# Hybrid attention and Hyena encoder on one core: the low parts of 72 weight chunks move from GpSimd to VectorE, 40 softmax divisions move from VectorE to ScalarE, eight rotary-table products get a second factor

## The chip, the cores and the metric

One core of a Trainium2 chip runs the whole program. The metric is the device time of one execution in microseconds (us). PE is TensorE, DVE is VectorE, ACT is ScalarE, POOL is GpSimd, SP is SyncE, whose queue starts most transfers here.

## The reference, cut to what matters

Two layers over 272 tokens (16 learned meta tokens and 256 of the input) of width 2048, all in fp32. Each layer has a latent attention with 8 heads beside a Hyena group (three streams, a short convolution, a long convolution by FFT), one output projection, and a SwiGLU network of inner width 5632. The meta tokens are dropped at the end, so the second layer computes mostly 256 tokens.

```
p = hn @ w_in[l]
a = mla(p[..., :o1], p[..., o1:o2], p[..., o2:o3], ...)   # 8 heads
y = hyena(p[..., o3:], ...)                               # v*x1, long conv, *x0
mix = concat([rmsnorm(a, attn_out_g[l]), rmsnorm(y, hy_out_g[l])])
h = h + mix @ w_out[l]
...
s = einsum('bqhd,bkhd->bhqk', qb, k) * scale
p = softmax(s)                                            # exp, then / sum
o = einsum('bhqk,bkhd->bqhd', p, v)
```

## The kernel before, in words

**Products in three parts.** TensorE multiplies fp32 numbers in a rounded form (fp32r). To keep the precision each operand is split: a high part, which ScalarE writes by a cast to fp32r (line 122), and a low part, which is the source minus the high part (line 123). `mm3` (lines 167 to 170) then gives three matmuls for each 128x128 block of a weight: high times high (L168), weight-high times activation-low (L169) and weight-low times activation-high (L170). So TensorE can't finish a block before both parts of its weight are there.

**The stream of weights.** All large weights pass through `Parts`. `load_raw` has SP load one tile of 128 rows and up to 2048 columns into one of four raw buffers; `more` splits it in chunks of 512 columns, four to a `u` tile (columns of w_in) and two to a `wo` tile (w_out), into six high and six low buffers. The transfers, the casts and the low parts are each held in the stream's order by a chain. The low part is made on VectorE, except where a chunk's number is in the argument `pool`: those go to GpSimd and are in no chain. For the 24 `u` tiles of a layer that argument is the table's entry `uw`: chunks 1 and 3 in layer 0 (48 instructions), chunk 1 in layer 1 (24). VectorE makes the other 120.

**What sets the order.** `drive` advances the stream (`fill`: 24 `u` tiles, then 16 `wo` tiles for the attention's half of w_out) one tile a round and, beside it, a number of threads: the latents, four pairs of heads (`pair`), the convolution's tables (`conv_tables`) and four convolution groups. The table `SCHED` (lines 47 to 50) says at which round each starts and how many rounds lie between its steps. From that the framework's scheduler lays out one fixed program for each engine, so an instruction that is late holds up all that stands behind it on the same engine.

**A `u` tile** (`stream_tile`) takes 48 matmuls into one of three PSUM buffers. L608 on VectorE evicts it (times the norm's factor), L609 on ScalarE and L610, L612 on VectorE make the short convolution. The third tile after it needs its PSUM buffer.

**Softmax** (`softmax`, called by `scores` in `pair`): VectorE scales the scores (L478), takes the row maximum (L479) and scales it (L480), ScalarE makes the exponential with the row sum (L481), VectorE the reciprocal (L482) and the product with it (L483). Then TensorE transposes p (`turn`, L562). There are three blocks of queries a head in layer 0 (24 calls) and two in layer 1 (16).

**Rotary tables** (`rope_tables`, L406 and L407): GpSimd multiplies the cosine and sine tables by a gain for each partition; two calls a layer, so eight instructions.

**The convolution** begins with `conv_tables`: ScalarE and VectorE split the tables of the Fourier transform, `ftw` into `fth` and `ftl`, `frw` into `fr`, `itw` last. `conv_group` makes filters (`fb`, `rt`, `ru`, `av`, of which L751, L753 and L759 are on GpSimd), their parts (`kl`, `ar`, `br`) and spectra (`KR`, `KP`).

Of the kernel before, what the change touches and what calls it, by code (L numbers as in the profile page):

```python
# [11 lines left out]
AF = mybir.ActivationFunctionType  # L12
ALU = mybir.AluOpType
# [31 lines left out]
NFIRST = 1  # L45
QV = 3
SCHED = (
    dict(lat=1, nets=0, pair=(4, 4, 11, 11), tab=16, conv=(14, 15, 17, 18), gq=1, gp=2, gt=3, gl=1, gw=2, gm=1, gf=3, gk=2, gu=3, gy=2, uw=(1, 3), fe=1),
    dict(lat=0, nets=0, pair=(2, 6, 9, 11), tab=14, conv=(12, 17, 17, 22), gq=2, gp=2, gt=1, gl=1, gw=2, gm=1, gf=1, gk=2, gu=2, gy=2, uw=(1,), fe=1),
)  # L50


# [1 line left out]
def tile_hybrid_encoder(ctx: ExitStack, tc: tile.TileContext, a: dict):  # L54
    nc = tc.nc
# [33 lines left out]
    def HT(name, dt=F32):  # L89
        return heap.tile([P, T], dt, tag="t1", name=nm(name))  # L90

    def SM(name):
        return smallp.tile([P, 1], F32, tag="s1", name=nm(name))
# [16 lines left out]
    cosT = cpool.tile([P, T], F32, name="cosT")  # L110
    sinT = cpool.tile([P, T], F32, name="sinT")

    def pc(l, c):
        return par[:, l * NP + c : l * NP + c + 1]
# [239 lines left out]
    for l in range(NL):  # L354
# [48 lines left out]

        def rope_tables(cg, cgs):
            cg_, sg_ = HT("cg"), HT("sg")
            nc.gpsimd.tensor_scalar(out=cg_, in0=cosT, scalar1=pc(l, cg), scalar2=None, op0=ALU.mult)  # L406
            nc.gpsimd.tensor_scalar(out=sg_, in0=sinT, scalar1=pc(l, cgs), scalar2=None, op0=ALU.mult)  # L407
            return cg_, sg_

        def rope(src, tabs, t0):  # L410
# [28 lines left out]
        for c, (c0, c1) in enumerate(CH):  # L439
            n = c1 - c0  # L440
# [21 lines left out]
        def latents():  # L462
            at["qla"] = latent_norm(qlc, qls, q0, C_GQL, 512, "ql")
            ktab = rope_tables(C_KR, C_KRS)
            at["qtab"] = rope_tables(C_QR, C_QRS)
            krot = rope(kr, ktab, 0)
            khi, klo = HT("krh", F32R), HT("krl", F32R)
            split(khi, klo, krot)
            at["krot"] = (khi, klo)
            at["krsq"] = HT("krsq")  # L470
            nc.scalar.activation(at["krsq"], kr, AF.Square)
            yield

        def softmax(ps, n, rk, rq, name):

            mx, sm = SM("mx"), SM("sm")
            p = HT(name)
            nc.vector.tensor_tensor(out=p[:n], in0=ps[:n, :T], in1=rk[:n], op=ALU.mult)  # L478
            nc.vector.tensor_reduce(out=mx[:n], in_=p[:n], axis=AX.X, op=ALU.max)  # L479
            nc.vector.tensor_scalar(out=mx[:n], in0=mx[:n], scalar1=rq[1][:n], scalar2=None, op0=ALU.mult)  # L480
            nc.scalar.activation(p[:n], p[:n], AF.Exp, bias=mx[:n], scale=rq[0][:n], accum_out=sm[:n])  # L481
            nc.vector.reciprocal(out=sm[:n], in_=sm[:n])  # L482
            nc.vector.tensor_scalar(out=p[:n], in0=p[:n], scalar1=sm[:n], scalar2=None, op0=ALU.mult)  # L483
            return p

        def pair(pr):
# [53 lines left out]
            def scores(j):  # L540
                ps_ = []
                kh, kl = ke[j][:2]
                qh, ql = qe[j][:2]
                for c, (s0, s1) in enumerate(qch):
                    n = s1 - s0
                    o = j * nq + c
                    ps = PA("s")
                    pw = ps[:n, :T]
                    MM(pw, lhsT=qr[j][:, s0:s1], rhs=at["krot"][0], start=True, stop=False)
                    MM(pw, lhsT=qr[j][:, s0:s1], rhs=at["krot"][1], start=False, stop=False)  # L550
                    mm3(pw, qh[:, s0:s1], ql[:, s0:s1], kh, kl, False, True)
                    ps_.append(softmax(ps, n, rk[j], (rq[:, o : o + 1], rqn[:, o : o + 1]), "p"))
                return ps_
# [566 lines left out]
```

## Time and profile before

| | |
|---|---|
| median of 3 runs | 2399.38 us (2398.22 to 2399.62) |
| the profiled execution's own time | 2399.11 us |
| its span | 2397.3 us |
| mean granted TensorE clock | 0.994 of full speed |
| PE / DVE / ACT / POOL busy | 98% / 69% / 54% / 20% |

The span is the stretch between the first and the last instruction on record; 1.8 us of the profiled execution lie around it. The program has, in this order, a start (to about 60 us), the streams with attention of layer 0 (to 260 us), its convolution (to 320 us), the rest of w_out and the wide network (to 1280 us), and the same again for layer 1 from 1280 us, with its streams and attention to 1460 us and its convolution to 1540 us. Everything that the change touches directly lies between 60 and 320 us and between 1280 and 1540 us.

To read it: the busy time of an engine in a stretch beside that stretch's length says how much room it has; the waits of PE say who came last when PE stood still; the granted clock says at which of its two levels, 2.4 GHz (1.0) and 1.2 GHz (0.5), TensorE ran, as a mean over the stretch.

### The profile page before, as it was taken

To read this page: it belongs to the slowest core of one execution; us is meant where nothing else is said; L and a number is where in the kernel's file an instruction comes from. 1 tells how busy PE (TensorE), PEld (TensorE's weight loads), DVE (VectorE), ACT (ScalarE), POOL (GpSimd) and SP (SyncE) were. 2 spreads that over 40 slices of the span, in tenths; PEclk is the share of its full clock that TensorE was granted. 3 is DMA by queue.
4 is the path that set the end of the run, shared out by engine and by line. 5 is a ranking of instruction groups with operands and counts; after the bars stand their busy time and mean duration, and the time that the engine had idled before them with its cause. 6 is when DMAs were issued, how large, how long until landed. Compare 5 with 4: busy or idle time off the path is not lost.

```text
span 2397.3 us, 48489 instructions
## 1 busy us (share of the span) xinstructions
PE 2357.8 (98%) x19026; PEld 2336.5 (97%) x19026; DVE 1644.7 (69%) x2997; ACT 1295.8 (54%) x2609; POOL 474.0 (20%) x564
## 2 busy tenths in 40 slices
PE   8999899999999999999999999899999999999999
PEld 7999899999999999999999999899999999999999
DVE  6898998755555555555667899997666655556555
ACT  6877565644444444444556776556445454445443
POOL 2645732211111100110013444431000010000000
PEclk9999999999999999999999999999999999999999
DMA  6434333555555555555454443246555555555554
GB/s 240 159 124 144 116 110 110 208 176 176 176 176 176 176 176 176 176 176 176 159 194 161 157 149 122 90 131 214 192 179 192 181 189 185 185 189 181 193 170 149
DMA packets 72938, 402.03 MB, mean 168 GB/s; under 512 B 8195, under 2 KB 18692, under 8 KB 33156
## 3 DMA queue, kind: packets, MB, share of 16 engines
q1 hardware_dynamic: 72152, 398.38, 49.0%
q8 instruction: 149, 2.44, 0.4%
q14 instruction: 81, 0.66, 0.1%
q10 hardware_dynamic: 556, 0.55, 0.1%
HBM read 396.79 MB, written 2.10 MB: 166 GB/s over the span
## 4 chain that ended last, share of the span: by engine, by line
PE 92%; DVE 5%; issue 1%; ACT 1%; DMA 1%; SPq 0%; DVEq 0%; ACTq 0%
PE fd L169 7%; PE fu L168 7%; PE fg L168 7%; PE fd L170 7%; PE fd L168 7%; PE fu L170 7%; PE fg L170 7%; PE fg L169 7%; PE fu L169 7%; PE u L168 3%; PE u L169 3%; PE u L170 3%; PE wo L168 3%; PE wo L169 3%; PE wo L170 2%
## 5 line engine op out<-in xcount | busy, mean ns | idle before, releaser
L169 PE MATMUL fd<-al,wdh 128*128 128x272 f32 (+1 forms) x1408 | 401.5, 285 | 0.0
L168 PE MATMUL fu<-nfh,wuh 128*128 128x272 f32 (+1 forms) x1408 | 401.1, 285 | 0.0
L168 PE MATMUL fg<-nfh,wgh 128*128 128x272 f32 (+1 forms) x1408 | 400.9, 285 | 0.0
L170 PE MATMUL fd<-ah,wdl 128*128 128x272 f32 (+1 forms) x1408 | 400.8, 285 | 0.0
L170 PE MATMUL fg<-nfh,wgl 128*128 128x272 f32 (+1 forms) x1408 | 400.5, 284 | 0.0
L170 PE MATMUL fu<-nfh,wul 128*128 128x272 f32 (+1 forms) x1408 | 400.5, 284 | 0.0
L168 PE MATMUL fd<-ah,wdh 128*128 128x272 f32 (+1 forms) x1408 | 400.2, 284 | 0.0
L169 PE MATMUL fu<-nfl,wuh 128*128 128x272 f32 (+1 forms) x1408 | 400.1, 284 | 0.0
L169 PE MATMUL fg<-nfl,wgh 128*128 128x272 f32 (+1 forms) x1408 | 400.0, 284 | 0.0
L123 DVE TENSOR_TENSOR wgl<-wg,wgh 128x512 fp32r<-128x512 f32 x352 | 244.1, 694 | 211.7 <-ACT wgh L122 203.4
L123 DVE TENSOR_TENSOR wdl<-wd,wdh 128x512 fp32r<-128x512 f32 x352 | 245.6, 698 | 199.1 <-ACT wdh L122 187.0
L122 ACT CAST wdh<-wd 128x512 fp32r<-128x512 f32 x352 | 218.5, 621 | 282.2 <-PE fd L169 263.1
L123 DVE TENSOR_TENSOR wul<-wu,wuh 128x512 fp32r<-128x512 f32 x352 | 260.5, 741 | 160.8 <-ACT wuh L122 154.6
L122 ACT CAST wgh<-wg 128x512 fp32r<-128x512 f32 x352 | 218.6, 621 | 262.0 <-PE fg L169 140.7
L122 ACT CAST wuh<-wu 128x512 fp32r<-128x512 f32 x352 | 218.5, 621 | 257.1 <-PE fu L169 138.6
L898 POOL TENSOR_TENSOR gt<-gt,up 128x272 f32<-128x272 f32 (+1 forms) x88 | 96.9, 1101 | 1113.5 <-ACT wuh L122 1053.1
L169 PEld LDWEIGHTS fu<-nfl,wuh 128*128 128x128 f32 x1408 | 265.6, 189 | 0.1
L169 PEld LDWEIGHTS fg<-nfl,wgh 128*128 128x128 f32 x1408 | 265.6, 189 | 0.0
L168 PEld LDWEIGHTS fd<-ah,wdh 128*128 128x128 f32 x1408 | 265.6, 189 | 0.0
L168 PEld LDWEIGHTS fu<-nfh,wuh 128*128 128x128 f32 x1408 | 265.5, 189 | 0.0
L168 PEld LDWEIGHTS fg<-nfh,wgh 128*128 128x128 f32 x1408 | 265.5, 189 | 0.0
L169 PEld LDWEIGHTS fd<-al,wdh 128*128 128x128 f32 x1408 | 265.4, 188 | 0.0
(372 smaller groups left out, 5871.6 us busy)
## 6 DMA issues: line engine op xcount, KB each, us to landing
wg<-w_gate SPq DMA_DIRECT2D x88, 1024.0 KB
wu<-w_up SPq DMA_DIRECT2D x88, 1024.0 KB
wd<-w_down SPq DMA_DIRECT2D x64, 1024.0 KB
u<-w_in SPq DMA_DIRECT2D x48, 1024.0 KB
wo<-w_out SPq DMA_DIRECT2D x64, 512.0 KB
wd<-w_down SPq DMA_DIRECT2D x32, 768.0 KB
ql<-w_in SPq DMA_DIRECT2D x8, 1024.0 KB
wq<-w_qk SPq DMA_DIRECT2D x8, 1024.0 KB
```

Of the source, the lines that this page charges most:

```text
L122: h_ = nc.scalar.copy(out=hi, in_=src)
L123: l_ = (nc.gpsimd if pool else nc.vector).tensor_tensor(out=lo, in0=src, in1=hi.bitcast(F32), op=ALU.subtract)
L168: MM(ps, lhsT=lh, rhs=rh, start=first, stop=False)
L169: MM(ps, lhsT=lh, rhs=rl, start=False, stop=False)
L170: MM(ps, lhsT=ll, rhs=rh, start=False, stop=last)
L898: nc.gpsimd.tensor_tensor(out=t[:, w], in0=t[:, w], in1=u[:, w], op=ALU.mult)
```

## The change

Three edits. The table's `uw` becomes empty in both layers, so that the 72 low parts that GpSimd made are made on VectorE, and join its chain. The softmax's L483 becomes a copy on ScalarE with the reciprocal as its scale (40 instructions). The eight products of the rotary tables get a second factor of 1.0.

```
-    dict(lat=1, ..., gy=2, uw=(1, 3), fe=1),
-    dict(lat=0, ..., gy=2, uw=(1,), fe=1),
+    dict(lat=1, ..., gy=2, uw=(), fe=1),
+    dict(lat=0, ..., gy=2, uw=(), fe=1),
...
-            nc.gpsimd.tensor_scalar(out=cg_, in0=cosT, scalar1=pc(l, cg), scalar2=None, op0=ALU.mult)
-            nc.gpsimd.tensor_scalar(out=sg_, in0=sinT, scalar1=pc(l, cgs), scalar2=None, op0=ALU.mult)
+            nc.gpsimd.tensor_scalar(out=cg_, in0=cosT, scalar1=pc(l, cg), scalar2=1.0, op0=ALU.mult, op1=ALU.mult)
+            nc.gpsimd.tensor_scalar(out=sg_, in0=sinT, scalar1=pc(l, cgs), scalar2=1.0, op0=ALU.mult, op1=ALU.mult)
...
-            nc.vector.tensor_scalar(out=p[:n], in0=p[:n], scalar1=sm[:n], scalar2=None, op0=ALU.mult)
+            nc.scalar.activation(p[:n], p[:n], AF.Copy, scale=sm[:n])
```

No other line differs, but the scheduler lays the engines' programs out anew. Three places show how; + is the changed kernel, - the one before.

DVE in layer 0, ahead of the eviction of one `u` tile (`u_4039`), among the transform's tables (`ftl`); `ul_4411` is the low part of a chunk of a later `u` tile, `wol_4558` that of a chunk of the first `wo` tile:

```order
+L123 TENSOR_TENSOR ul_4411<-u_4400,uh_4410 128x512
+L123 TENSOR_TENSOR ul_4415<-u_4400,uh_4414 128x512
 L123 TENSOR_TENSOR ftl_3949<-ftw_3551,fth_3948 128x256
-L123 TENSOR_TENSOR ul_4231<-u_4220,uh_4230 128x512
 L123 TENSOR_TENSOR ftl_3953<-ftw_3553,fth_3952 128x256
+L123 TENSOR_TENSOR wol_4558<-wo_4555,woh_4557 128x512
 L123 TENSOR_TENSOR ftl_3957<-ftw_3555,fth_3956 128x256
 L123 TENSOR_TENSOR ftl_3961<-ftw_3557,fth_3960 128x256
+L123 TENSOR_TENSOR wol_4562<-wo_4555,woh_4561 128x512
 L123 TENSOR_TENSOR ftl_3965<-ftw_3559,fth_3964 128x256
 L608 TENSOR_TENSOR u_4039<-u_3972,nmr_505 128x272
-L123 TENSOR_TENSOR ul_4403<-u_4400,uh_4402 128x512
```

The low parts of the stream stand further ahead against the convolution's work than before, and four of 128x512 stand in this piece ahead of the eviction where one stood.

ACT in layer 0, in the softmax of the first heads; `uh_2358` and its like are casts of the stream, `uc_2061` is the short convolution of a `u` tile:

```order
-L122 CAST uh_2219<-u_2205 128x512
 L122 CAST uh_2358<-u_2356 128x512
+L122 CAST uh_2362<-u_2356 128x512
+L483 ACTIVATE p_1911<-p_1911,sm_1910 128x272
+L609 ACTIVATE uc_2061<-u_2060,par 128x272
 L481 ACTIVATE p_1926,sm_1925<-p_1926,mx_1924,rq_1703 128x272
-L122 CAST uh_2362<-u_2356 128x512
+L122 CAST uh_2366<-u_2356 128x512
 L481 ACTIVATE p_1941,sm_1940<-p_1941,mx_1939,rq_1703 16x272
-L609 ACTIVATE uc_2061<-u_2060,par 128x272
-L122 CAST uh_2366<-u_2356 128x512
+L483 ACTIVATE p_1926<-p_1926,sm_1925 128x272
```

The scaled copies stand among the stream's casts, and one cast more stands ahead of each exponential.

SP in layer 0, where the tables of the convolution's remainder (`frw`) are loaded among the stream's tiles:

```order
 L137 DMA dec_3820<-dec 50x256
 L137 DMA skip_3822<-skip 18x256
+L142 DMA wo_4804<-w_out 128x1024
 L137 DMA frw_3940<-rdft 96x256
 L137 DMA frw_3942<-rdft 96x256
 L137 DMA frw_3944<-rdft 96x256
 L137 DMA frw_3946<-rdft 96x128
-L142 DMA wo_4705<-w_out 128x1024
-L142 DMA wo_4804<-w_out 128x1024
 L142 DMA wo_4980<-w_out 128x1024
```

The loads of `frw` now stand behind two more tiles of the stream (`wo_4705`, which stands earlier now, and `wo_4804`); in layer 1 they stand behind two more `u` tiles.

## Rows read from the trace of the kernel before

**Rows 1.** Page: busy time by engine; shares of the chain that ended last.

```profile
PE 2357.8 (98%) x19026; PEld 2336.5 (97%) x19026; DVE 1644.7 (69%) x2997; ACT 1295.8 (54%) x2609; POOL 474.0 (20%) x564
PE 92%; DVE 5%; issue 1%; ACT 1%; DMA 1%; SPq 0%; DVEq 0%; ACTq 0%
```

**Rows 2.** Busy time in four stretches; the first line names the columns.

```profile
core 0: us, PE busy (x) PEld busy (x) DVE busy (x) ACT busy (x) POOL busy (x), PEclk, DMA share, GB/s
60.00:260.00 200.00, 196.83 (x1529) 188.31 (x1528) 173.11 (x402) 150.79 (x364) 108.17 (x109) 1.00 0.42 145
260.00:320.00 60.00, 49.48 (x358) 47.72 (x357) 57.72 (x96) 30.07 (x75) 44.97 (x60) 0.91 0.33 107
1280.00:1460.00 180.00, 179.09 (x1441) 177.32 (x1440) 158.19 (x347) 133.83 (x323) 80.16 (x89) 1.00 0.47 160
1460.00:1540.00 80.00, 68.04 (x497) 65.93 (x496) 72.94 (x145) 45.14 (x125) 39.03 (x69) 0.89 0.28 89
```

**Rows 3.** Waits of PE: who waited for whom, us total, times, longest.

```profile
PE u L168 <- DVE u L608: 7.5, 3, 5.6
PE wo L168 <- DVE u L608: 3.8, 2, 3.4
PE KR L688 <- DVE ar L698: 3.5, 1, 3.5
PE pt L562 <- DVE p L483: 1.0, 3, 0.4
```

**Rows 4.** Groups by line, all run: count, busy us, mean ns, idle before.

```profile
L123 POOL TENSOR_TENSOR ul<-u,uh 128x512 fp32r<-128x512 f32 x72 | 100.4, 1394 | 131.9 <-ACT uh L122 116.9 <-DVE ul L123 5.4 <-PE u L170 4.7
L123 DVE TENSOR_TENSOR ul<-u,uh 128x512 fp32r<-128x512 f32 x120 | 98.7, 824 | 16.4 <-ACT uh L122 15.1 <-PE pt L562 0.5
L123 DVE TENSOR_TENSOR wgl<-wg,wgh 128x512 fp32r<-128x512 f32 x352 | 244.1, 694 | 211.7 <-ACT wgh L122 203.4
L483 DVE TENSOR_SCALAR p<-p,sm 128x272 f32<-128x272 f32 (+1 forms) x40 | 20.2, 508 | 0.3
L130 ACT ACTIVATE nmh<-h,par 128x272 fp32r<-128x272 f32 x32 | 16.2, 520 | 5.8 <-DMA h<-xT 3.4 <-DMA par<-par 2.4
```

**Rows 5.** Busy in stretches, tile ul alone; columns PE, PEld, DVE, POOL.

```profile
260.00:320.00 60.00, 19.32 (x66) 12.81 (x66) 8.21 (x10) 9.19 (x6) 0.91 0.33 107
1460.00:1540.00 80.00, 21.56 (x76) 14.58 (x76) 8.97 (x22) 4.05 (x3) 0.89 0.28 89
```

**Rows 6.** Timeline of POOL, 271 to 281 us: start, duration, what.

```profile
271.18 3.06 POOL L759 TENSOR_TENSOR av<-fb,fb 128x256 f32<-128x256 f32 x4
...
274.89 1.27 POOL L123 TENSOR_TENSOR ul<-u,uh 128x512 fp32r<-128x512 f32 x1
...
277.25 1.43 POOL L123 TENSOR_TENSOR ul<-u,uh 128x512 fp32r<-128x512 f32 x1
```

**Rows 7.** Timeline of DVE in the same stretch.

```profile
273.56 3.15 DVE L123 TENSOR_TENSOR ul<-u,uh 128x512 fp32r<-128x512 f32 x1
276.63 4.06 DVE L123 TENSOR_TENSOR ftl<-ftw,fth 128x256 fp32r<-128x256 f32 x4
280.73 0.44 DVE L608 TENSOR_TENSOR u<-u,nmr 128x272 f32<-128x272 f32 x1
```

**Rows 8.** Busy in stretches, line 483 alone; first column DVE.

```profile
60.00:260.00 200.00, 12.96 (x24) 1.00 0.42 145
1280.00:1460.00 180.00, 7.20 (x16) 1.00 0.47 160
```

**Rows 9.** Tile sg: count, shortest, median, longest ns, first and last start.

```profile
L407 POOL TENSOR_SCALAR sg<-sinT,par x4: 1049/1495/1607, 96.8 to 1299.1; 128x272 f32<-128x272 f32 x4
```

**Rows 10.** Tile frw, the same columns.

```profile
L137 SPq DMA_DIRECT2D frw<-rdft x8: 318/376/474, 263.7 to 1438.1; - x8
L655 ACT CAST fr<-frw x8: 297/403/404, 303.8 to 1458.6; 96x256 fp32r<-96x256 f32 x6, 96x128 fp32r<-96x128 f32 x2
```

**Rows 11.** Timeline of SP behind those loads in layer 1.

```profile
1443.35 7.79 SPq L142 DMA_DIRECT2D u<-w_in  x2
```

More of the change, by code (lines that the diff above doesn't have):

```diff
@@ L47 @@
 SCHED = (
-    dict(lat=1, nets=0, pair=(4, 4, 11, 11), tab=16, conv=(14, 15, 17, 18), gq=1, gp=2, gt=3, gl=1, gw=2, gm=1, gf=3, gk=2, gu=3, gy=2, uw=(1, 3), fe=1),
-    dict(lat=0, nets=0, pair=(2, 6, 9, 11), tab=14, conv=(12, 17, 17, 22), gq=2, gp=2, gt=1, gl=1, gw=2, gm=1, gf=1, gk=2, gu=2, gy=2, uw=(1,), fe=1),
+    dict(lat=1, nets=0, pair=(4, 4, 11, 11), tab=16, conv=(14, 15, 17, 18), gq=1, gp=2, gt=3, gl=1, gw=2, gm=1, gf=3, gk=2, gu=3, gy=2, uw=(), fe=1),
+    dict(lat=0, nets=0, pair=(2, 6, 9, 11), tab=14, conv=(12, 17, 17, 22), gq=2, gp=2, gt=1, gl=1, gw=2, gm=1, gf=1, gk=2, gu=2, gy=2, uw=(), fe=1),
 )
```

## The prediction

> **What bounds the kernel now.** I read the busy times first. TensorE is busy 98% of the span and 92% of the chain that ended last is TensorE's [rows 1]. A change on the other three engines can therefore gain only where TensorE stands still or runs at its low clock, and can lose anywhere it makes TensorE wait. So next comes the table by stretch [rows 2]: busy time subtracted from length gives 3.2 us of idle TensorE in 60 to 260 us, 10.5 in 260 to 320, 0.9 in 1280 to 1460 and 12.0 in 1460 to 1540. The clock is full in the two attention stretches and 0.91 and 0.89 in the two with the convolution; set against full clock that is 60 x 0.09 = 5.4 and 80 x 0.11 = 8.8 us of clock. VectorE is busy 57.7 of 60 and 72.9 of 80 us there, but has 26.9 and 21.8 us to spare in the attention stretches. ScalarE has 49 and 46 us to spare in those two. The waits say the same by name: the longest are those for L608, the eviction of a `u` tile, and for the split of the filters' remainder, L698, both on VectorE [rows 3]. So the kernel is bound by TensorE nearly everywhere, and by VectorE around the two convolutions. What the change does to VectorE there decides.
>
> My sum is made against the profiled execution's own 2399.11 us, 0.27 us under the median of the runs, which is inside their spread.
>
> **Low parts in the attention stretches.** Of the 72 low parts, 9 are GpSimd's in the convolution stretches (6 and 3 [rows 5]), so 63 lie in the attention stretches. A low part of this size costs VectorE 0.694 us where GpSimd has little to do (the weights of the wide network), 0.824 in the `u` tiles where it has much, and 1.394 on GpSimd [rows 4]. I take 0.69, since the operations that collided leave with the change. That adds 63 x 0.69 = 43.5 us. The division takes 12.96 + 7.20 = 20.2 us from VectorE, all of it in the attention stretches [rows 8]. Net 23.3 us against 26.9 + 21.8 = 48.7 to spare: it fits, even with nothing won back elsewhere. What hides it is VectorE's slack; without it the whole 23 us would be on the path. TensorE is idle 4.1 us here in all [rows 2] and I let 1.0 of it come back, because low parts that took 1.394 us will take half. Bounds: -2 (half of that idle time) to +4 (it doubles).
>
> **Low parts in the convolution stretches.** Nine low parts add 9 x 0.69 = 6.2 us to an engine that is full. Against that, 9.19 + 4.05 = 13.2 us of the same work leave GpSimd [rows 5], and VectorE visibly stands still beside GpSimd: at 273.56 one low part takes 3.15 us instead of 0.69, and the next four small ones 4.06 us, while GpSimd runs without a gap from 271.18 [rows 6, 7]. The eviction that TensorE waits for comes right behind them, at 280.73. How much of GpSimd's time VectorE loses can't be read from a row exactly. Nothing lost gives +6.2; all 13.2 lost gives 6.2 - 13.2 = -7.0. I take half, 6.6, as other GpSimd work (the `av` sums [rows 6]) stays and can stop VectorE in place of what left: -0.4 us. Half is a choice between the two ends, not a reading.
>
> **Division on ScalarE.** 40 copies at 0.52 us, by the nearest row, a scaled copy of 128x272 [rows 4], are 20.8 us in stretches where ScalarE has 95 us to spare. As a duration it is no gain against the 0.508 on VectorE [rows 4]; what counts is where it queues. In the new order the copy stands among the stream's casts, and it needs VectorE's reciprocal, so the casts behind it wait too, and the low parts behind these, and TensorE's third product. Cover: six high and six low buffers ahead of TensorE. TensorE waits for p 1.0 us in all now [rows 3]. I take +0.3. Bounds: -1.0 (that wait goes) to +8.3 (each of the 16 batches of one head's scores is 0.52 later).
>
> The Trainium skill, "ScalarE: Activation LUTs", section "Rules for kernel authors", says to use VectorE and not ScalarE for a plain multiplication, for its higher rate in bf16. This case's data are fp32, and the two rows give 508 and 520 ns: no difference here. By the page the edit would be a loss of time on ScalarE, but idle time hides it.
>
> **Rotary tables.** Eight GpSimd products of 1.05 to 1.61 us [rows 9], with a second factor. If the second multiplication took another pass, each would take about as long again, and `sg` and `cg` of a call follow one another ahead of the rotation. Two calls in a layer are four products, but only the first two stand ahead of the keys' rotation; about +2.6 us a layer, +5 in all. I take 0: no row shows a second pass, and GpSimd has 87 us less of `ul` to make in the attention stretches, where they stand (100.4 [rows 4] less the 13.2).
>
> **Order.** The loads of `frw` stand two stream tiles later on SP. In layer 0 they were issued at 263.7 and first used at 303.8 us; in layer 1 the last at 1438.1, and two `u` loads are issued within 7.79 us, by 1451.2, against a last use at 1458.6 [rows 10, 11]. That leaves 7 us in the tighter one, so 0. On VectorE the eviction of `u_4039` stands behind four low parts more than half a stream tile further on: 4 x 0.69 = 2.8 us later if VectorE is late there. These four must be made at some time and are then missing from the queue behind it, so TensorE gets the time back at a later tile: 0, bounds 0 to +2.8 a layer.
>
> **Sum:** -1.0 - 0.4 + 0.3 + 0 + 0 + 0 = -1.1, so 2399.1 - 1.1 = 2398.0 us.
>
> **Rivals.**
>
> *Faster: the blocking is complete.* If VectorE loses all of the time that GpSimd's low parts run, the convolution stretches get 7.0 us back. That is 7.0 of their 22.5 us of idle TensorE, 31%; if the low clock follows the idle time, 31% of 5.4 + 8.8 comes back too, 4.4 us. Together -11.4: 2388 us. For it: the 3.15 us row, and the 0.824 against 0.694. Against it: in that very stretch GpSimd's `av` work stays [rows 6], and 3.5 us of the waits are for the remainder's chain [rows 3], which has steps on other engines.
>
> The Trainium skill, "SBUF — State Buffer", section "Who interferes with whom", states this as a rule: VectorE and GpSimd share a pair of ports under an exclusive lock, and the one that starts first stops the other. By that, every microsecond of a GpSimd operation is lost to a two-operand VectorE operation that meets it, which is this rival. The trace agrees that VectorE is stopped (3.15 against 0.69) but not that all of GpSimd's time is lost.
>
> *Slower: VectorE at the evictions.* If nothing is won back, the nine low parts cost 6.2 us, and the four that stand ahead of an eviction come on top, 2.8 us in each layer: 6.2 + 5.6 = +11.8, 2411 us. It decides from the point where the low parts in the queue ahead of L608 delay it past the end of the two tiles that TensorE has in hand; before, that happened five times [rows 3]. For it: VectorE is 96% and 91% busy in these stretches. Against it: the 3.15 us.
>
> *Slower: ScalarE's copy on the path of the scores.* The +8.3 of above: 2407 us. It decides if VectorE, which makes the reciprocal behind the stream's low parts, is late. For it: VectorE is now fuller in the attention stretches (in layer 0, with 42 of the 63, 173.1 + 42 x 0.69 - 13.0 = 189 of 200 us). Against it: the transposes stand a tile of stream work behind.
>
> *It doesn't do what it says:* the nine low parts of the convolution stretches could move into the attention stretches with the new order. Then the change is worth nothing either way: 2399.4.
>
> **How the numbers follow.** About 0.2%, 4.8 us, is what a measurement of this kernel can tell from no change; that is 2394.6 to 2404.2. Chances: forecast 0.43, blocking 0.30, evictions 0.17, scores 0.07, nothing 0.03. The forecast's own range is 2393 to 2405, by the bounds of the convolution's term; of its 0.43 some 0.05 end under 2394.6 and 0.02 over 2404.2. Of the blocking's 0.30 some 0.28 end under. Faster: 0.28 + 0.05 = 0.33. Slower: 0.17 + 0.07 - 0.01 + 0.02 = 0.25. Same: the rest, 0.42. For the range I cut the rivals: 2386 leaves out 0.08 of the blocking, 2410 leaves out 0.11 of the evictions.
>
> **What the changed profile would show.** No `ul` on GpSimd, 192 on VectorE with a mean under 0.75 us (over 0.85 would refute the relief). VectorE's busy time in the attention stretches near 189 and 165 us. In the convolution stretches, VectorE's busy time no higher than before if half of the blocking holds, and the wait for L608 near 11 us; under 6 us with a clock over 0.95 is the faster rival; over 17 us is the slower. L483 on ScalarE near 0.52 us and the wait of the transposes under 2 us; over 5 is the rival with the scores. L406 and L407 between 1.0 and 1.6 us; twice that refutes the 0. The prediction is wrong if TensorE's idle time in the four stretches moves by over 5 us from 26.6, or their clocks by over 0.03.

## The result: slower by 0.56%, and the profile after

The changed kernel takes 2412.65 us (median of 4 runs, 2411.62 to 2413.43) against 2399.18 in the same comparison: a ratio of 1.0056 with an interval of 1.0043 to 1.0069, or +13.5 us. The forecast was 2398.0 and the range ended at 2410. The profiled execution took 2411.62 us, its span 2409.7, so 12.4 us of span are to be found. (Executions that were disturbed and ran far longer are left out of the ratios; one of them was the profiled one of e1_low below, so that kernel was run again as e1b_low.)

The page's busy times and shares of the chain, for [rows 1]:

```profile
PE 2361.3 (98%) x19026; PEld 2338.1 (97%) x19026; DVE 1644.6 (68%) x3029; ACT 1313.7 (55%) x2649; POOL 380.9 (16%) x492
PE 93%; DVE 3%; ACT 2%; issue 1%; DMA 1%; POOL 0%; SPq 0%; DVEq 0%; ACTq 0%; POOLq 0%
```

VectorE has 32 more instructions (72 low parts came, 40 divisions went) and the same busy time, 1644.6 against 1644.7 us. So VectorE did not become fuller, and still the kernel is slower. The four stretches, for [rows 2], with the same columns:

```profile
60.00:260.00 200.00, 196.48 (x1524) 188.20 (x1523) 172.69 (x409) 159.12 (x384) 51.54 (x66) 1.00 0.42 143
260.00:320.00 60.00, 46.90 (x332) 44.76 (x331) 55.00 (x105) 27.25 (x62) 34.94 (x52) 0.89 0.35 111
1280.00:1460.00 180.00, 178.05 (x1389) 174.09 (x1387) 149.46 (x323) 133.93 (x317) 45.29 (x62) 0.99 0.46 159
1460.00:1540.00 80.00, 63.35 (x472) 59.80 (x471) 73.95 (x156) 45.73 (x119) 36.36 (x59) 0.94 0.30 95
```

TensorE stands idle 3.5 + 13.1 + 2.0 + 16.7 = 35.2 us in them, against 26.6 before. Its waits, for [rows 3]:

```profile
PE u L168 <- DVE u L608: 7.9, 2, 7.4
PE wo L168 <- DVE u L608: 5.3, 2, 4.6
PE pt L562 <- ACT p L483: 4.8, 3, 2.4
PE KR L688 <- DVE ar L698: 3.4, 2, 2.3
PE KP L168 <- DVE fb L738: 3.0, 1, 3.0
```

The transposes wait 4.8 us where they waited 1.0, the evictions 13.2 where they took 11.3, and a wait for the filters, L738, is new. The groups, for [rows 4], and the two rotary products, for [rows 9]:

```profile
L123 DVE TENSOR_TENSOR ul<-u,uh 128x512 fp32r<-128x512 f32 x192 | 144.5, 757 | 23.4 <-ACT uh L122 21.6 <-PE u L170 0.2
L483 ACT ACTIVATE p<-p,sm 128x272 f32<-128x272 f32 (+1 forms) x40 | 20.5, 515 | 0.8 <-DVE sm L482 0.7
```

```profile
L406 POOL TENSOR_SCALAR cg<-cosT,par x4: 490/492/1608, 86.8 to 1297.5; 128x272 f32<-128x272 f32 x4
L407 POOL TENSOR_SCALAR sg<-sinT,par x4: 668/861/943, 87.3 to 1298.0; 128x272 f32<-128x272 f32 x4
```

The change did what it says. The copies took 0.515 us where 0.52 was taken, and the tables mostly became shorter. The low parts took 0.757 us in the mean, more than the 0.69 taken and just over the 0.75 that the prediction had named as a sign.

**Stage by stage.** The wide networks issue the same matmuls in the same order in every kernel here, and yet their lengths differ by some us between builds (last section). So the loss is read from the rest. A mixer is the part of a layer ahead of its wide network: mixer 0 runs from the first matmul of a `u` tile to the first of w_gate in layer 0, network 0 from there to the last of w_down, mixer 1 from there to the first of w_gate in layer 1 (with the norm between the layers, some 50 us in all of them), network 1 to the last of w_down. Starts of matmuls, from the traces of all kernels of this study, in us:

```
                  mixer 0  network 0  mixer 1  network 1   mixers against before
before              379.5     791.9     407.0     750.1
after               383.3     794.8     414.3     747.9      +11.1
e1b_low             386.1     793.8     404.8     749.0       +4.4
e2_div              380.0     796.5     411.8     745.7       +5.3
e3_rope             382.4     791.5     406.5     747.4       +2.4
e4_lowdiv           386.2     793.8     414.8     747.7      +14.5
p1_after_old        376.1     796.8     402.7     747.0       -7.7
p2_before_new       393.3     794.1     418.8     750.5      +25.6
p3_div_old          380.6     795.0     405.3     750.1       -0.6
p4_low_old          375.9     794.5     403.7     746.0       -6.9
r1_evict_first      382.5     795.4     414.4     748.9      +10.4
r2_new0_old1        383.2     794.8     403.9     747.5       +0.6
r3_lowrope_old      375.8     794.5     402.0     749.5       -8.7
r4_pe_old           379.8     792.9     409.1     749.7       +2.4
r5_dve_old          390.1     793.0     409.7     746.1      +13.3
r6_pedve_old        384.6     793.7     404.9     748.8       +3.0
r7_dve_free         381.7     794.5     408.2     751.3       +3.4
```

The changed kernel loses 3.8 us in mixer 0 and 7.3 in mixer 1; the rest of its 12.4 lies in the start (0.6) and the networks (0.7).

### The profile page after: what moved, and what is told of

It reads as the page before. It is cut to its first block, busy times and chain, and to the rows that moved or that the text cites. A ratio compares the mean times of both kernels' runs of the same rounds, so it can differ in the third digit from the quotient of the medians.

```text
span 2409.7 us, 48446 instructions
## 1 busy us (share of the span) xinstructions
PE 2361.3 (98%) x19026; PEld 2338.1 (97%) x19026; DVE 1644.6 (68%) x3029; ACT 1313.7 (55%) x2649; POOL 380.9 (16%) x492
## 4 chain that ended last, share of the span: by engine, by line
PE 93%; DVE 3%; ACT 2%; issue 1%; DMA 1%; POOL 0%; SPq 0%; DVEq 0%; ACTq 0%; POOLq 0%
PE fd L170 7%; PE fu L168 7%; PE fg L168 7%; PE fg L169 7%; PE fd L168 7%; PE fu L170 7%; PE fg L170 7%; PE fu L169 7%; PE fd L169 7%; PE u L168 4%; PE u L170 3%; PE u L169 3%; PE wo L168 2%; PE wo L169 2%; PE wo L170 2%
## 5 line engine op out<-in xcount | busy, mean ns | idle before, releaser
L170 PEld LDWEIGHTS fd<-ah,wdl 128*128 128x128 f32 x1408 | 264.9, 188 | 0.0
```

Source lines behind the costliest of these rows:

```text
L170: MM(ps, lhsT=ll, rhs=rh, start=False, stop=last)
```

## The experiments

### One edit at a time

e1_low has `uw=()` alone, e2_div the scaled copy alone, e3_rope the second factor alone, e4_lowdiv the first two. Their edits are lines of the change shown above:

```
e1_low   -uw=(1, 3) / uw=(1,)                      +uw=()
e2_div   -nc.vector.tensor_scalar(out=p[:n], ...)  +nc.scalar.activation(p[:n], p[:n], AF.Copy, scale=sm[:n])
e3_rope  -scalar2=None, op0=ALU.mult               +scalar2=1.0, op0=ALU.mult, op1=ALU.mult
```

e1_low. 

> Only the first edit: all low parts of the u tiles on VectorE; division on VectorE and rotary tables as before. The changed kernel lost 4.3 us around the convolution of layer 0 and 7 us in the last heads of layer 1. Theory L (low parts ahead of the evictions): both losses come from the low parts; this kernel loses about as much, +9 to +14 us, or more, since the 20 us of division stay on VectorE. Theory S (scaled copy on the scores' path): only layer 0's 4 us remain, +3 to +6. Theory R (any edit makes the scheduler lay out an order that the table was not chosen for): a loss of some us whose place need not be that of the changed kernel.

e2_div. 

> Only the second edit: division as a scaled copy on ScalarE. Theory L: within 3 us of before. Theory S: +5 to +8 us, with 4 to 5 us of TensorE waiting in the transposes for the scaled copy, in the last heads of layer 1. Theory R: a loss of some us, without the transposes' wait having to be its largest.

e3_rope. 

> Only the third edit: rotary tables with a second factor. In the changed kernel these eight GpSimd products were shorter (0.49 and 0.86 us as medians) than before (1.20 and 1.50 us). If the second factor is what makes them shorter, they are near 0.5 to 0.9 us here too; if it was GpSimd's emptier stretch, they stay at 1.2 to 1.5. Theories L and S: within 2 us of before. Theory R: the order differs in 641 lines on TensorE, and the time may move by several us either way.

e4_lowdiv. 

> First and second edit without the third: the changed kernel with the old rotary tables. Theories L and S: as the changed kernel, +12 to +14 us, with the sum of the two single losses. Theory R: the third edit redraws the order too, so the time may differ from the changed kernel's by several us, and the single losses need not add up.

Ratios to the kernel before (2399.73 us there): e1_low 1.0030 (1.0018 to 1.0042), about +7 us; e2_div 1.0026 (1.0016 to 1.0037), +6; e3_rope 0.9992 (0.9984 to 1.0001), no difference that can be told; e4_lowdiv 1.0053 (1.0040 to 1.0066), +13. The two losses add up, and the third edit is nearly nothing. Neither L nor S holds by itself: the +7 of e1_low lies between what S (+3 to +6) and L (+9 to +14) had for it, and the +6 of e2_div is past the 3 us of L. Each could still hold for its part. The table by stage sets them apart: the low parts alone (e1b_low) lose 6.6 us in mixer 0 and gain 2.2 in mixer 1, the division alone loses 0.5 and 4.8.

e1b_low. 

> The first edit alone again, for an undisturbed profile: about 2405, with the loss over the kernel before in the mixer of layer 0, of layer 1 or both; by the pinned runs the low parts themselves gain, so the loss must show as waits that the new order puts in (evictions L608, transposes).

It took 2404.61 us (one run, no interval). Waits of TensorE in e1b_low, then in e2_div:

```profile
PE u L168 <- DVE u L608: 12.3, 4, 7.3
PE pt L562 <- DVE p L483: 1.6, 2, 1.2
```

```profile
PE u L168 <- DVE u L608: 7.9, 3, 6.1
PE pt L562 <- ACT p L483: 3.5, 4, 1.3
```

With the low parts moved, the evictions of the `u` tiles are waited for (12.3 us against 7.5 in [rows 3]); with the division moved, the transposes (3.5 against 1.0). These look like the two slow rivals of the prediction. But each edit also made the scheduler redraw the order: even e3_rope, which moves nothing between engines, differs from the kernel before in 204 lines of TensorE's trace (the shortest difference of the two, buffer numbers left out; 982 lines for the changed kernel) and has a mixer 0 that is 2.9 us longer. Work and order had to be parted.

### The new work in the old order, and the old work in the new order

In these kernels every instruction is pinned, engine by engine, behind the one that it shall follow, from a table of the instructions' names in the order of another kernel's program:

```
+    for n in order_of_the_other_program:
+        i = have["I-%d" % n]
+        if i.engine in last:
+            tc.add_manual_dep(i, last[i.engine], DependencyInfo(NoSync, DATA), reason="pinned order")
+        last[i.engine] = i.name
```

It adds an order and no wait. A moved instruction enters its new engine's row at the place in the program at which the other kernel issued it. The traces bear it out: TensorE's 19026 instructions in p1_after_old stand in the order of the kernel before, ScalarE's row differs by the 40 copies alone, VectorE's by the 72 low parts and the 40 products.

p1_after_old. 

> The changed kernel's work in the order of the kernel before: on each engine every instruction is pinned behind the one it stood behind before; the 72 low parts and the 40 scaled copies are let into their new engines' rows at the place in the program at which they were issued before. The three single edits gave +7.2, +6.3 and -2 us, together about the +13.5 of the whole change. Theory O (the order that the scheduler makes of the new work is what costs): this kernel loses at most 3 us and may gain. Theory W (the work on its new engine is what costs: low parts ahead of evictions because VectorE has more to do, scaled copies on the scores' path): +9 to +14 us as the changed kernel.

p2_before_new. 

> The other way round: the work of the kernel before (72 low parts on GpSimd, division on VectorE) in the changed kernel's order. Theory O: +8 us or more. Theory W: within 3 us of before.

p3_div_old. 

> Only the division moved to ScalarE, all else pinned to the order before. By itself, in the order that the scheduler made, it cost 6.3 us. Theory O: within 2 us of before. Theory W: +5 to +7, with 3 to 5 us of TensorE waiting in the transposes for the scaled copy.

p4_low_old. 

> Only the low parts moved to VectorE, all else pinned to the order before. In the scheduler's order it cost 7.2 us. Theory O: within 2 us of before or below. Theory W: +6 to +9, with longer waits for the evictions L608.

Against 2399.64 us: p1_after_old 2393.69, ratio 0.9975 (0.9965 to 0.9985); p2_before_new 2428.03, 1.0116 (1.0101 to 1.0132); p3_div_old 2400.71, 1.0008 (0.9999 to 1.0017); p4_low_old 2389.54, 0.9958 (0.9945 to 0.9970). Theory W falls, and theory R of the single edits, for which the third edit had given little sign, is what is left: with theory O it says the same. The very work that is 13.5 us slower in its own order is 6 us faster in the old one: the order costs about 19 us, and the edits themselves are worth -6. The low parts alone gain 10 us there, the division by itself is worth nothing that can be told. The old work suffers from the new order more than the new work does (+28 us).

The four stretches of p1_after_old, and its waits:

```profile
60.00:260.00 200.00, 198.25 (x1548) 190.77 (x1547) 178.53 (x420) 161.18 (x388) 55.21 (x74) 1.00 0.44 148
260.00:320.00 60.00, 50.62 (x366) 48.82 (x366) 56.73 (x109) 32.03 (x85) 31.42 (x59) 0.91 0.32 103
1280.00:1460.00 180.00, 178.56 (x1433) 176.29 (x1432) 158.07 (x351) 138.12 (x334) 47.02 (x67) 1.00 0.47 160
1460.00:1540.00 80.00, 69.93 (x538) 67.94 (x537) 73.72 (x156) 47.69 (x133) 38.19 (x69) 0.94 0.27 89
```

```profile
PE u L168 <- DVE u L608: 4.3, 2, 4.0
PE wo L168 <- DVE u L608: 3.8, 2, 3.4
PE pt L562 <- ACT p L483: 0.5, 1, 0.5
```

TensorE is idle 1.8 + 9.4 + 1.4 + 10.1 = 22.6 us, 4.0 less than before, and the last stretch has a clock of 0.94 instead of 0.89, by an estimate 80 x 0.05 = 4.0 us more. Together 8.0, against 7.7 in the mixers. With the same scaled copies on ScalarE the transposes wait 0.5 us here and 4.8 in the changed kernel. And in p2_before_new, where the division is back on VectorE, they still wait 5.9 us:

```profile
PE pt L562 <- DVE p L483: 5.9, 2, 3.3
```

So neither slow rival is a property of the moved work.

### What in the order costs

In mixer 1 it can be seen on TensorE. For the sixteen heads in turn, the number of TensorE instructions between the last score matmul of a head and the first transpose of its p, which is what covers the softmax:

```
before, p1  75 109 55 59 63 101 50 69 | 96 59 50 138 69 62 58 60
e1_low     103 144 53 49 87 133 53 70 | 96 59 50 150 79 88 70 30
e2_div      79 129 52 56 63 118 54 74 | 96 65 60 152 83 93 39 30
after, p2   91 132 57 60 83 132 54 79 | 96 69 67 151 84 94 25 25
```

The changed kernel has more cover for most heads, and 25 instead of 58 and 60 for the last two of layer 1. There TensorE waits. The changed kernel's timeline of TensorE, VectorE and ScalarE at the last head (start, duration, in brackets the idle time before and its releaser):

```profile
1468.43 0.29 PE L549 MATMUL s<-krh,qr 128*128 128x272 f32 x1
...
1476.96 0.55 PE L562 MATMUL pt<-ident,p 128*128 128x128 f32 x3 [2.25 <-ACT p L483]
```

```profile
1471.92 0.43 DVE L478 TENSOR_TENSOR p<-s,knr 128x272 f32<-128x272 f32 x1
...
1476.19 0.16 DVE L482 RECIPROCAL sm<-sm 128x1 f32<-128x1 f32 x1
```

```profile
1474.50 0.61 ACT L481 ACTIVATE p<-p,mx,rq 128x272 f32<-128x272 f32 x1 [2.79 <-DVE mx L480]
...
1476.38 0.52 ACT L483 ACTIVATE p<-p,sm 128x272 f32<-128x272 f32 x1 [0.68 <-DVE sm L482]
```

The second block's scores are done at 1469.2 us. VectorE takes them up at 1471.9, behind the first block's steps and two low parts of the stream; in this time it stands idle for 1.1 us, for the first block's exponential and for a cast of the stream. Between its further steps stand the filters' `fb`, `rt` and `ru`, so its reciprocal comes at 1476.2, the scaled copy ends at 1476.9, and the transposes have waited 2.25 us. The copy itself is 0.52 us of these 7.7. ScalarE stands still for 2.79 us ahead of the exponential, with the stream's casts queued behind it.

In mixer 0 the prediction had named a place, the eviction of `u_4039` behind four low parts. It is there:

```profile
281.79 1.95 DVE L123 TENSOR_TENSOR ul<-u,uh 128x512 fp32r<-128x512 f32 x2
283.66 1.82 DVE L123 TENSOR_TENSOR ftl<-ftw,fth 128x256 fp32r<-128x256 f32 x2
285.40 1.20 DVE L123 TENSOR_TENSOR wol<-wo,woh 128x512 fp32r<-128x512 f32 x1
286.53 0.75 DVE L123 TENSOR_TENSOR ftl<-ftw,fth 128x256 fp32r<-128x256 f32 x2
287.20 0.68 DVE L123 TENSOR_TENSOR wol<-wo,woh 128x512 fp32r<-128x512 f32 x1
287.80 0.41 DVE L123 TENSOR_TENSOR ftl<-ftw,fth 128x256 fp32r<-128x256 f32 x1
288.24 0.44 DVE L608 TENSOR_TENSOR u<-u,nmr 128x272 f32<-128x272 f32 x1
```

```profile
288.83 0.57 PE L168 MATMUL u<-nmh,uh 128*128 128x272 f32 x1 [7.38 <-DVE u L608]
```

r1_evict_first pins the changed kernel's own order and puts these four behind the eviction:

```
 ftl_3965<-ftw_3559,fth_3964
 L608 u_4039<-u_3972,nmr_505
+ul_4411, ul_4415, wol_4558, wol_4562      (before: between the ftl, ahead of L608)
```

r1_evict_first. 

> The changed kernel, its own order pinned on every engine, with one difference: on VectorE the four low parts ul_4411, ul_4415, wol_4558 and wol_4562 stand right behind the eviction L608 of u_4039 in layer 0 instead of ahead of it. They took 3.8 us there (1.95 + 1.20 + 0.68), and TensorE waited 7.4 us for that eviction. If what stands ahead of the eviction costs time that is not given back: 3 to 5 us faster than the changed kernel, about 2408 to 2410. If, as the prediction had it, TensorE gets that time back at a later tile anyway: within 1 us of the changed kernel's 2412.7.

It took 2411.97 us, ratio 1.0047 (1.0033 to 1.0060), within 1 us of the changed kernel. Its waits:

```profile
PE u L168 <- DVE u L608: 5.0, 1, 5.0
PE KP L168 <- DVE fb L738: 3.0, 1, 3.0
```

The wait shrank from 7.4 to 5.0 us, and mixer 0 by 0.8. TensorE stood 2.1 us ahead at the 24 `wo` matmuls just ahead of the wait for the filters, and left the same wait for the filters 0.6 us ahead. The columns of [rows 2] over these matmuls and that wait, in the changed kernel and then in r1_evict_first:

```profile
306.60:312.90 6.30, 3.29 (x26) 3.06 (x24) 6.04 (x14) 5.38 (x14) 1.05 (x2) 1.00 0.69 211
304.47:312.28 7.81, 4.80 (x27) 4.58 (x25) 6.14 (x14) 5.38 (x14) 1.05 (x2) 0.75 0.60 178
```

The matmuls took 1.5 us longer, at a granted clock of 0.75 instead of 1.00, and TensorE still waited 3.0 us: VectorE, with the four low parts now behind the eviction, had the filters ready only 0.6 us earlier. So nearly all of the time was given back, as that one sentence of the prediction said. One eviction is not the cause. And this kernel pins the changed kernel's own order and takes its time within 1 us, so the pinning itself costs nothing that can be told.

r2_new0_old1 has the new order to the middle of network 0 and the old one from there.

r2_new0_old1. 

> The changed kernel's work, in its own order up to the middle of layer 0's wide network and in the order of the kernel before from there on. All old gave 2393.7, all new 2412.7. By the traces the new order is behind the old one by about 9 us at the end of layer 0's mixer and by 8 to 10 us more in layer 1. If the two layers' losses are separate: about 2402 to 2404. If layer 0's order alone makes the loss, and layer 1 is late only by what comes before it: about 2412.

2400.48 us, ratio 1.0002 (0.9993 to 1.0011): the losses of the two layers are separate, 6.8 us over p1_after_old for layer 0 (383.2 against 376.1 in its mixer) and 12 for layer 1.

The last four pin only some engines of the changed kernel's work to the old order and leave the others to the scheduler.

r4_pe_old. 

> The changed kernel's work with TensorE alone pinned to the order before; the scheduler lays out the other engines around that. In the changed kernel the scores and their transposes stand nearer to each other on TensorE in the last heads of layer 1 (about 33 to 58 matmuls between, 69 to 110 before), and the eviction of u_4039 is one with four low parts ahead of it on VectorE. If TensorE's order is what costs: within 4 us of the all-old 2393.7, at most 2398. If the other engines' orders cost (low parts ahead of evictions): nearer to the changed kernel, over 2403.

r5_dve_old. 

> The changed kernel's work with VectorE alone pinned to the order before, the other engines laid out by the scheduler around it. All old gave 2393.7, TensorE alone old 2403.0, all new 2412.7. If VectorE's order carries the rest of the loss: 2394 to 2400. If the loss sits in how TensorE's and ScalarE's rows stand to it: over 2403.

r6_pedve_old. 

> TensorE and VectorE pinned to the order before, ScalarE, GpSimd and SP laid out by the scheduler. If these two orders are what costs, and they had to go together: 2392 to 2397, as all old. If ScalarE's order, where the scaled copies and exponentials stand among the casts, has a share: 2398 to 2404, with waits of the transposes for p.

r7_dve_free. 

> TensorE, ScalarE, GpSimd and SP pinned to the order before, VectorE laid out by the scheduler. If VectorE's order costs by itself: 2398 to 2404. If the order of the others settles it: 2392 to 2397.

Ratios: TensorE alone 1.0015 (1.0006 to 1.0024); VectorE alone 1.0040 (1.0026 to 1.0054); both 1.0012 (1.0003 to 1.0021); all but VectorE 1.0010 (1.0001 to 1.0019); all, p1_after_old, 0.9975. The first, 2402.97 us, lies at the edge of the second case set for it (over 2403); the second says that VectorE's old order alone is no cure, the third that ScalarE's order has a share, the fourth that VectorE's has. So no single engine's order holds the loss. TensorE's gives back half (9.7 of 19 us), and the last 8 to 9 us come only when all are old. With TensorE alone in the old order the cover of 58 and 60 instructions is back, and yet the transposes wait longer than ever for the scaled copies, since the softmax's steps on VectorE and ScalarE stand where the scheduler puts them around that order:

```profile
PE pt L562 <- ACT p L483: 9.6, 7, 3.8
```

### The fastest kernel

r3_lowrope_old. 

> All low parts on VectorE and the rotary tables with a second factor, the division left on VectorE, all pinned to the order before: the first edit alone in that order gave 2389.5, 10 us under the kernel before. If the shorter rotary products also help there: 2387 to 2389. If they are hidden: 2389 to 2390. This would be the fastest of all so far in either case.

b1_low_old. 

> The same kernel as p4_low_old (low parts on VectorE, order before) on one chip with the next: 2389 to 2392 if its first result holds.

b2_lowrope_old. 

> The same kernel as r3_lowrope_old (with the rotary tables' second factor). On another chip it was 4 us behind p4_low_old, though its mixers were 2 us shorter and only stretches without any change were longer. If that was the chip or the execution: within 2 us of b1_low_old. If the second factor costs in this order: 3 to 5 us behind.

r3_lowrope_old took 2393.60 us (0.9972, 0.9961 to 0.9984), over both of the ranges set for it. On one chip, the low parts alone in the old order took 2390.91 (0.9963, 0.9950 to 0.9975), with the second factor 2393.77 (0.9971, 0.9959 to 0.9982). The 2.9 us between them lie between the two cases set. The intervals overlap, so it is not shown that the second factor costs 3 us; no gain is seen. What would hold these 3 us is network 1, 746.0 against 749.5 us in both pairs of profiles, where the two kernels run the same instructions. The kernel that beats both is the first edit in the old order, about 9 to 10 us under the kernel before in both of its comparisons.

## Why the prediction was wrong

**The step that failed is "Order", costed at 0 with bounds of 0 to +2.8 us a layer.** It measured +7.2 us in mixer 0 (383.3 against 376.1) and +11.6 in mixer 1 (414.3 against 402.7), the changed kernel against the same work in the old order. The two mixers of the changed kernel and then of p1_after_old, with the columns of [rows 2]:

```profile
66.08:449.35 383.27, 366.64 (x2845) 355.89 (x2843) 338.75 (x757) 262.76 (x635) 125.27 (x178) 0.98 0.40 132
1244.14:1658.48 414.34, 395.15 (x3133) 387.13 (x3132) 355.36 (x754) 272.00 (x647) 124.70 (x182) 0.98 0.42 143
64.22:440.30 376.08, 364.94 (x2844) 355.51 (x2843) 340.50 (x757) 262.35 (x635) 120.99 (x178) 0.99 0.40 135
1237.09:1639.78 402.69, 390.94 (x3133) 384.32 (x3132) 352.36 (x754) 270.34 (x647) 120.93 (x182) 0.99 0.44 147
```

VectorE is busy within 3 us of the same, but TensorE is idle 16.6 and 19.2 us against 11.1 and 11.8: 12.9 of the 18.8 us. The prediction's own signs fired too: the idle time of the four stretches moved by 8.6 us where 5 had been set, and the last one's clock by 0.05 where 0.03 had been set. I had looked at three places of a redrawn program and priced these; at the one on VectorE the pricing held (r1_evict_first). But 982 lines of TensorE's trace had changed, and in layer 1 the cost lay where I had not looked: in how near the last heads' transposes stand to their scores (they wait 4.8 us, 0.5 in the old order), and in how VectorE's and ScalarE's rows stand to that.

**Low parts in the attention stretches: -1.0.** The sign was right and the size too small. TensorE's order is the same in p4_low_old and before, so stretches can be cut at the same matmuls there: the two of the attention are 197.6 and 180.1 us long, 200.0 and 180.0 before, together 2.3 us shorter and a little past the bound of -2. What I had called the cover, VectorE's slack, was hardly used: the changed kernel's VectorE is busy 172.7 and 149.5 us there and p1_after_old's 178.5 and 158.1, where I had said 189 and 165. Over the whole program the 72 low parts should have added 72 x 0.69 = 50 and the division taken 20.2 away; busy time did not change, so 29.8 us of standing still went away with 100.4 us of GpSimd work. With the first edit alone in the old order it is more: p4_low_old's VectorE is busy 1653.5 us, 8.8 more than before, so about 41 of the 50 went away.

**Low parts in the convolution stretches: -0.4, by half of 13.2 us.** These two stretches in p4_low_old, cut at the matmuls that stand at 260, 320, 1460 and 1540 us before:

```profile
258.44:317.20 58.76, 49.90 (x358) 48.13 (x356) 56.45 (x105) 29.95 (x74) 33.59 (x52) 0.91 0.35 109
1459.87:1536.75 76.88, 65.42 (x498) 63.42 (x497) 70.19 (x149) 46.00 (x126) 34.60 (x65) 0.93 0.28 92
```

They are 1.2 and 3.1 us shorter than 60 and 80, where -0.4 was forecast. VectorE is busy 4.0 us less than in [rows 2] with nine more low parts, about 6.2 us, so about 10 of the 13.2 us came back: half was too little, and the rival's all was nearer. In the second stretch the gain is mostly clock, 0.93 instead of 0.89, by an estimate 80 x 0.04 = 3.2 us. Both mixers of p4_low_old together are 6.9 us shorter (in its profiled execution, which at 2391.54 us is 2.0 over its median), and with all three edits 7.7, against the -1.1 of the sum. The faster rival had these two parts, blocking and clock. In time p1_after_old, 2393.7 us, lies between the forecast and that rival.

The Trainium skill, "SBUF — State Buffer", section "Who interferes with whom", has VectorE and GpSimd share ports under an exclusive lock. The traces agree in kind: before, the 59 low parts of `u` tiles on VectorE that meet no GpSimd instruction take at most 0.695 us, and the 61 that meet one take 0.96 us in the mean and up to 3.15. In amount the 100.4 us taken from GpSimd gave VectorE 30 to 41 us back; why not more was not tried.

**Division on ScalarE: +0.3.** Right for the work: p3_div_old is 0.6 us shorter in its mixers and 1.0008 in its ratio. ScalarE's copy took 0.515 us where 0.52 was taken. In the changed kernel the transposes wait 4.8 us, just under the 5 that I had set for the rival with the scores; that rival's mechanism, a copy 0.52 us long on the path, is refuted by p1_after_old, which has the same copies and 0.5 us of wait, and by p2_before_new, which has none and 5.9.

**Rotary tables: 0.** Right in its effect, wrong in its bounds: I had thought of a longer product and it became shorter (last section).

**The slow rival at the evictions: 2411.** Nearest in time, by luck: its mechanism is not the cause. Its first price, VectorE too full, fails by the busy times; its second, the four low parts, by r1_evict_first for the one place that was tried.

**What stays open.** Which places of the order hold the 7.2 us of layer 0: one was tried, and it was not the cause. How much of the 11.6 us of layer 1 the short cover makes by itself: no run moved the last heads' transposes alone. And why the scheduler draws a worse order for the new work. Its plan is not in the profile, and the kernel's table of starts and gaps stood as it was for the old work. No run here tried another table for the new work.

## What to carry to other kernels

In a kernel whose program is laid out by a scheduler, an edit is two changes: the work, and a new order for all engines. Part them by pinning one kernel's order on the other's work before judging either; here they were worth -6 and +19 us. When an order is compared by eye, look also at how much TensorE work stands between a producer and its consumer (scores and transposes), and at where the steps between them stand on the other engines: with TensorE's order alone put back, the transposes waited longer still.

## What the runs showed of the hardware that was not expected

**A GpSimd product with a scalar for each partition is shorter with a second factor of 1.0.** The kernels p4_low_old and r3_lowrope_old differ in that alone and have the same order. Tiles cg and sg in p4_low_old, then in r3_lowrope_old (count, shortest, median, longest ns):

```profile
L406 POOL TENSOR_SCALAR cg<-cosT,par x4: 977/1130/1360, 85.5 to 1290.7; 128x272 f32<-128x272 f32 x4
L407 POOL TENSOR_SCALAR sg<-sinT,par x4: 971/1234/2381, 86.7 to 1292.0; 128x272 f32<-128x272 f32 x4
```

```profile
L406 POOL TENSOR_SCALAR cg<-cosT,par x4: 488/600/744, 85.3 to 1289.9; 128x272 f32<-128x272 f32 x4
L407 POOL TENSOR_SCALAR sg<-sinT,par x4: 667/858/941, 86.0 to 1290.4; 128x272 f32<-128x272 f32 x4
```

In e3_rope, where GpSimd still makes its 72 low parts, the effect is smaller: the median of cg falls from 1.20 to 0.68 us, that of sg from 1.50 to 1.23.

**The same matmuls take a little longer in one build than in another.** In the networks TensorE never waits and its clock is full. In network 1 the mean step from one matmul to the next is 118.40 ns before, 118.06 after, 117.76 in p4_low_old and 118.31 in r3_lowrope_old, the same again in the second profile of each of the last two, on other chips; over 6336 matmuls 0.55 ns are 3.5 us. What differs between the builds there was not tried. It is as large as some of the effects that this study looked for, and it is why the losses were read from the mixers.
